# Query tile 5 of the B heads turned by VectorE and DRAM, and the order's offsets set per stage

## The chip, the core and the metric

The kernel runs on one core of a Trainium2 chip. The metric is the device time of one execution in microseconds. TensorE (PE) multiplies matrices and turns 128x128 blocks, VectorE (DVE), ScalarE (ACT) and GpSimd (POOL) work on elements, and SyncE (SP) issues every DMA of this kernel. Each engine takes its instructions in the order in which the program holds them.

## The reference, cut to what matters

One layer over 1024 prompt tokens and 32 sample tokens, model width 1024:

```python
u = rmsnorm(h, g_pre) @ w_in            # q k v g of A (8 heads x 64) and of B (8 heads x 64)
oA = band attention                     # softmax(q k / 8 + relative bias), own 64-frame chunk and 8 before it
oB = stick_breaking(q, k, v)            # strictly causal:
z = q @ k.T * ATTN_SCALE
log_beta = log_sigmoid(z)
log_1m = where(causal, log_sigmoid(-z), 0)
after = cumsum(log_1m, reverse=True) - log_1m
w = where(causal, exp(log_beta + after), 0);  o = w @ v
y = concat(oA * silu(gA), oB * silu(gB)) @ w_out
h = h + rmsnorm(y, g_post)
h = h + sigmoid(h @ w_ple_gate) * (p @ w_ple)
```

The outputs are y of both groups and their new keys and values. In the kernel the weight of stick-breaking is a product: sigmoid(z) times the running product of sigmoid(-z) from the right.

## The kernel before, in words

Every product runs in fp32r, with an operand split into a high and a low part where precision asks for it (names ending in h and l). The input projections are done column by column (`col_steps`), 128 columns of w_in for 1056 tokens in three chunks of 352, 24 matmuls a chunk (`mm_qA`, `mm_kB`, `mm_gB` and so on).

Attention runs pair by pair of heads, A and B in turn (`pairs`: A0, B0, A1, ... B3), two heads a pair, eight query tiles a head. For query tile i `scores(i)` makes the scores in PSUM (`S`, three banks). For B, ScalarE makes two sigmoids into `om` and `be`, VectorE runs the scan in `om`, and GpSimd multiplies into `be`. For A, VectorE adds the bias and takes the extremum, ScalarE takes exp, GpSimd scales. Then `weights_t(i)` must turn the weights, so that keys lie on the partitions. There are two ways:

- on TensorE: a transpose of each 128x128 block into PSUM (`ptw`, two banks), after which ScalarE copies the high part (`wTh`) and VectorE subtracts for the low part (`wTl`);
- for the query tiles in `ROUND`: VectorE transposes all 32x32 blocks of the tile into `om`, one DMA writes `om` to a scratch tensor in DRAM (`swap`), and four DMAs read it back into `be` with the blocks in their new places. ScalarE and VectorE then make `wTh` and `wTl` from `be`.

Before, `ROUND` holds tile 5 of A's heads and tiles 4 and 6 of B's. Tile i of a B head has i+1 blocks of 128 keys. `values(g)` multiplies the turned weights of queries 4g to 4g+3 with the values (`PV`). `om` and `be` lie in rings (`Arena`), so that a later tile's room waits for the last use of an earlier one.

`weave` sets the attention steps of a pair beside the projections that the next pair needs: it takes from the list whose share of done work is behind, weighed by `RATES`, with the estimates of `SPACE_S`, `SPACE_T` and `SPACE_V` for the attention steps. `with_sums` puts in sums of the late weights at the places of `SUMS_STEP`, `with_sample` the steps of the sample group at `SAMPLE_AT`. After attention come the last gates, then the output product `o` and the gate product `g`, each with seven block products.

No instruction is issued directly. `Recorder.add` notes each one with what it must wait for and a key, which is its place in the recording (and a class: `cls` for TensorE, `low` for the others). `order()` then plays the program through with assumed durations and gives each engine, whenever it is free, the ready instruction of the lowest key. So the key decides which of several ready instructions goes first. `AHEAD_OF` shifts the key of instructions by engine and name of the tile written: a negative number lets it go earlier, a positive one later. Before, it does not touch TensorE:

```python
if eng != "PE" and writes:
    name = str(writes[0].buf.name)
    kind = (eng, name[:next(...)])
    o.key = (o.key[0], o.key[1] + AHEAD_OF.get(kind, 0))
```

Names in the profile: every instruction has line 490, where the recorder emits it, so groups are told apart by tile names. A trailing A or B tells the mixer.

Of the kernel before, what the change touches and what calls it, by code (L numbers as in the profile page):

```python
# [25 lines left out]
SCALE = HD ** -0.5  # L26
NT = 9
AHEAD_OF = {
    ('ACT', 'L'): 100, ('ACT', 'Qfs'): 50, ('ACT', 'stq'): 400, ('ACT', 'x'): -50,
# [3 lines left out]
}  # L33

ROUND = {"A": ((5,),), "B": ((4,),(6,))}
LAG_T = 2
LAG_V = 2
SPACE_S = {'A': 0.1, 'B': 0}  # L40
SPACE_T = {'A': 0.4, 'B': 0.4}
SPACE_V = {'A': 0.05, 'B': 0.0}
PARTS = 4
BEHIND = 2
RATES = (0.96, 0.86, 0.92, 1.0, 1.0, 0.86, 1.12, 0.86)
PLE_LAG = 4.0


# [6 lines left out]
class View:  # L55


    def __init__(self, buf, steps, box, dims, shape):
        self.buf, self.steps, self.box, self.dims, self.shape = buf, steps, box, dims, shape
# [213 lines left out]
class Recorder:  # L273


    def __init__(self):
        self.with_table, self.old_table = [], []
        self.ops, self.cls, self.low, self.closed, self.turns = [], 0, 0, [], []
        self.tensor = Engine(self, "PE", "tensor")
        self.vector = Engine(self, "DVE", "vector")  # L280
        self.scalar = Engine(self, "ACT", "scalar")
        self.gpsimd = Engine(self, "POOL", "gpsimd")
        self.sync = Engine(self, "SP", "sync")
# [26 lines left out]
    def node(self, eng, what, args, kw, after):  # L310
        o = Op()
        o.eng, o.what, o.args, o.kw, o.after = eng, what, args, kw, after
        o.key = (self.cls if eng == "PE" else self.low, len(self.ops))
        o.shared, o.table = False, None
        self.ops.append(o)
        return o

    def add(self, eng, what, args, kw):
        writes, reads = [], []
        method = what[1] if isinstance(what, tuple) else ""  # L320
        for i, a in enumerate(args):
            if isinstance(a, (View, Raw, Segments)):
                (writes if i == 0 or (method == "tensor_tensor_reduce" and i == 7) else reads).append(a)
        for k, a in kw.items():
            if isinstance(a, (View, Raw, Segments)):
                (writes if k in ("out", "accum_out") else reads).append(a)
        o = self.node(eng, what, args, kw, set())
        for mine, write in ((reads, False), (writes, True)):
            for v in mine:
                b = v.buf  # L330
                hit = False
                for other, box, wrote in b.uses:
                    if other is not o and (write or wrote) and all(p < y and x < q for (p, q), (x, y) in zip(v.box, box)):
                        o.after.add(other)
                        hit = True
                if b.pool is not None:
                    if not hit:
                        o.after.add(b.place)
                    b.pool.ops.append(o)
                b.uses.append((o, v.box, write))  # L340
        if method == "activation" and args[2] in (AF.Exp, AF.Sigmoid):

            o.table = args[2]
            if self.with_table and self.with_table[-1].table != o.table:
                self.old_table, self.with_table = self.with_table, []
            self.with_table.append(o)
            o.after.update(self.old_table)
        if eng != "PE" and writes:
            name = str(writes[0].buf.name)
            kind = (eng, name[:next((i for i, x in enumerate(name) if x.isdigit() or x in "AB_"), len(name))])  # L350
            o.key = (o.key[0], o.key[1] + AHEAD_OF.get(kind, 0))
        o.busy, o.late = self.cost(eng, method, args, kw, writes, reads)
        if eng == "SP":
            o.pieces = max(self.pieces(v) for v in args[0:2])
        o.shared = eng == "POOL"
        if eng == "DVE":
            sbuf = [v for v in reads if isinstance(v, (View, Segments)) and not v.buf.psum and v.free() > 4]
            o.shared = len(sbuf) > 1 or (method == "tensor_copy" and len(sbuf) == 1 and not writes[0].buf.psum)
# [137 lines left out]
def stream_step(  # L496
# [6 lines left out]
    rec = Recorder()  # L503
# [29 lines left out]
    hnl = [hnp.tile([P, KD, CH], F32R, tag=f"hnl{c}", name=f"hnl{c}") for c in range(NCH)]  # L533
# [14 lines left out]
    masks = const.tile([P, NS], F32, tag="masks", name="masks")  # L548
    qsS = const.tile([P, 4, NS], F32, tag="qsS", name="qsS")
    ksS = const.tile([P, 4, NS], F32, tag="ksS", name="ksS")  # L550
# [310 lines left out]
    def attention(ab, p, h):  # L861
# [15 lines left out]

        together = {i: g for g in ROUND[ab] for i in g}
        whole, done_with = {}, []

        def cost(i):
            return i + 1 - lo_block(i)
# [104 lines left out]
        def reach(g, b):  # L987

            seen = [i for i in range(4 * g, 4 * g + 4) if lo_block(i) <= b <= i]
            return slice((seen[0] - 4 * g) * P, (seen[-1] + 1 - 4 * g) * P)  # L990
# [23 lines left out]
        for i in range(8):  # L1014
            out["S", i] = (0.107 * cost(i) + SPACE_S[ab], lambda i=i: scores(i))
            out["T", i] = (0.107 * cost(i) + SPACE_T[ab], lambda i=i: weights_t(i))
        for g in range(2):
            columns = sum(reach(g, b).stop - reach(g, b).start for b in range(4 * g + 4))
            out["V", g] = (0.00088 * columns + SPACE_V[ab], lambda g=g: values(g))
        return out  # L1020
# [328 lines left out]
    def weave(n, att, den):  # L1349
# [5 lines left out]
        while ia < len(att) or idn < len(den):  # L1355
            take_a = ia < len(att) and (idn >= len(den) or RATES[n] * pa / ta <= pd / td)
            if take_a and att[ia][2] and any(x in prep for x in att[ia][2]):
# [52 lines left out]
                sub(b[key], b["B11"], b[key], ALU.subtract)  # L1410
                dma(sum_dr[w][kt, 3], b[key])

    SUMS_STEP = {2: [8, 34], 4: [10, 28], 5: [8, 28], 6: [14, 28]}

    def with_sums(n, att, todo):
        out = list(att)
        for i, (w, kt) in enumerate(todo):
            out.insert(SUMS_STEP[n][i], (0.0, lambda w=w, kt=kt: sum_weights(w, kt), None))
        return out

    SAMPLE_AT = {2: [0, 10, 16, 23, 26, 27], 3: [4, 10, 15, 22, 27, 32], 6: [1, 10, 15, 22, 27, 32], 7: [1, 9, 15, 22, 23, 32]}

    def with_sample(n, att, steps):
        out = list(att)
        for at_, st in reversed(list(zip(SAMPLE_AT[n], steps))):
            out.insert(at_, (st[0], st[1], None))
        return out
# [8 lines left out]
    grow = at2.tile([1, D], F32, tag="tok", name="grow", bufs=2)  # L1436
# [3 lines left out]
    ple = Ple(True)  # L1440
# [56 lines left out]

    seq = attention_stream()
    for n in range(8):
        den = []  # L1500
        for j in range(*span[n + 1]):
            den += col_steps(j)
        att = seq[n, 0] + seq[n, 1]
        if pairs[n][1] % 2 == 1:
            att = with_sample(n, att, sample_attention(pairs[n][0], pairs[n][1] // 2))
        att = with_sums(n, att, SUMS_AT.get(n, ()))
        weave(n, att, den)
# [2 lines left out]


    rec.close(at_stack, at)
    fb = rec.pool(ctx, tc, name="fb", bufs=1)
    GP = fb.tile([P, D], F32, tag="GP", name="GP")
    L, R = HALF
# [17 lines left out]
    ple = Ple(False)  # L1533
# [265 lines left out]

    for m, (nm, src, group) in enumerate(sets):  # L1800
        last_set = m == len(sets) - 1
        state = [{}, {}]
        for n, prod in enumerate(ORDER):
            for pair, t in enumerate(group):
# [43 lines left out]
                if nm == "o":  # L1848
                    rec.low = -1
                    if prod == "P2":  # L1850
                        add(st["h1u"][:, L], st["p1"], bank, ALU.add)
                        st["u"].square(0, st["h1u"][:, L])
                    if prod == "P6":
                        add(up, st["p1"], bank, ALU.add)
                    if prod == "P7":
                        add(dn, up, bank, ALU.add)
# [13 lines left out]
                else:  # L1870
                    uu = st.get("uu")
                    if prod in ("P2", "P4") and pair == 0:
                        name = f"cc{m}{prod}"
                        if m == 2 and prod == "P4":
                            cc = at2.tile([P, 2, 512], F32, tag="stg", name=name, bufs=3)
                        elif m == 3 and prod == "P2":
                            cc = at0.tile([P, 2, 512], F32, tag="L0", name=name)
                        else:
                            cc = fb.tile([P, 2, 512], F32, tag="GP", name=name)
# [76 lines left out]
```

## Time and profile before

| | |
|---|---|
| median of 3 runs | 783.63 us (783.26 to 783.88) |
| the profiled execution | 783.64 us |
| its span, first to last instruction | 781.9 us |
| granted clock of TensorE, mean | 0.999 |
| busy: TensorE / VectorE / ScalarE / GpSimd | 98% / 77% / 68% / 60% |
| moved by DMA | 154.71 MB, mean 198 GB/s |

A row of the groups reads: line, engine, operation, tile written <- tiles read, shapes, count, then busy time in us and the mean ns of one, then the idle time of the engine just before them and what ended it. The busy time of TensorE contains matmuls that overlap; what one costs is read from start to start. A line of the timeline has start and length in us, then the instruction and the count of a run of equal ones. The stretch from 50 to 575 us holds the attention and most of the gates, that before it the norms and the first projections, that behind it the last gates and the output and gate products.

### The profile page before, as it was taken

How to read it: one execution, taken by the hardware profiler on the slowest of the kernel's cores; microseconds unless marked ns; L12 is line 12 of the kernel's file. 1: busy time of each engine (PE TensorE's matmuls, PEld its weight loads, DVE VectorE, ACT ScalarE, POOL GpSimd, SP SyncE). 2: the span in 40 equal slices, each digit the busy share in tenths (PEclk: the TensorE clock that was granted, in tenths of full speed). 3: DMA queues.
4: the chain of work that ended last, by engine and by line, in shares of the span. 5: the costliest groups of instructions: out<-in, count | busy, mean ns of one | idle time of the engine just before them, and what ended most of it. 6: DMA issues, size and time to landing. Idle time of an engine off the chain costs nothing.

```text
span 781.9 us, 14437 instructions
## 1 busy us (share of the span) xinstructions
PE 769.8 (98%) x4534; PEld 711.2 (91%) x4534; DVE 602.9 (77%) x1127; ACT 528.4 (68%) x1146; POOL 471.7 (60%) x551
## 2 busy tenths in 40 slices
PE   8999999999999999999999999999999999999997
PEld 6999999999999999999999999999998877877786
DVE  7827767888778888688988798888474687988965
ACT  5647775877786777787767777674347867685651
POOL 5636624574666446775966677575553438599533
PEclk9999999999999999999999999999999999999999
DMA  8657634557765638776757977775689856659754
GB/s 301 215 152 180 161 82 139 136 128 210 177 196 167 183 92 240 185 213 210 197 143 199 260 209 218 197 223 167 184 276 289 274 181 220 239 160 346 250 181 134
DMA packets 184542, 154.71 MB, mean 198 GB/s; under 512 B 64705, under 2 KB 150505, under 8 KB 184466
## 3 DMA queue, kind: packets, MB, share of 16 engines
q1 hardware_dynamic: 184466, 153.79, 66.8%
q8 instruction: 36, 0.59, 0.3%
q14 instruction: 40, 0.33, 0.1%
HBM read 94.97 MB, written 50.36 MB: 186 GB/s over the span
## 4 chain that ended last, share of the span: by engine, by line
PE 80%; POOL 7%; DVE 4%; DMA 3%; issue 3%; SPq 2%; ACT 1%; POOLq 0%; DVEq 0%; ACTq 0%
PE mm_gB L490 6%; PE mm_qB L490 6%; PE mm_qA L490 5%; PE mm_vA L490 5%; PE mm_kA L490 5%; PE mm_vB L490 5%; PE mm_kB L490 4%; PE PVB L490 4%; PE SB L490 4%; PE PVA L490 3%; PE SA L490 3%; PE ptwA L490 3%; PE o1P L490 3%; PE g2P L490 2%; PE o0P L490 2%
## 5 line engine op out<-in xcount | busy, mean ns | idle before, releaser
L490 POOL TENSOR_TENSOR be<-be,om 128x256 f32<-128x256 f32 (+8 forms) x66 | 83.5, 1269 | 82.1 <-DVE om L490 48.9
L490 DVE TENSOR_TENSOR_SCAN om<-om,SB 128x384 f32<-128x384 f32 (+5 forms) x96 | 92.6, 968 | 20.2 <-ACT be L490 11.1
L490 ACT ACTIVATE om<-SB 128x384 f32<-128x384 f32 (+5 forms) x96 | 46.6, 499 | 23.8 <-DVE SB L490 12.5
L490 POOL TENSOR_SCALAR be<-be,statA 128x640 f32<-128x640 f32 (+4 forms) x64 | 46.0, 727 | 25.8 <-DVE statA L490 22.2
L490 ACT ACTIVATE be<-SB 128x384 f32<-128x384 f32 (+5 forms) x96 | 46.3, 500 | 13.2 <-DVE om L490 6.6
L490 ACT ACTIVATE be<-om,statA 128x640 f32<-128x640 f32 (+4 forms) x64 | 44.4, 695 | 5.9 <-DVE statA L490 3.9
L490 DVE TENSOR_TENSOR wTl<-ptwA,wTh 128x512 fp32r<-128x512 f32 (+2 forms) x80 | 37.2, 482 | 12.5 <-ACT wTh L490 11.4
L490 ACT CAST wTh<-ptwA 128x512 fp32r<-128x512 f32 (+2 forms) x80 | 32.2, 425 | 20.4 <-PE ptwA L490 19.1
L490 ACT CAST wTh<-ptwB 128x512 fp32r<-128x512 f32 (+3 forms) x64 | 29.8, 488 | 15.4 <-PE ptwB L490 10.7
L490 DVE TENSOR_TENSOR wTl<-ptwB,wTh 128x512 fp32r<-128x512 f32 (+3 forms) x64 | 33.5, 542 | 5.3 <-ACT wTh L490 4.9
L490 PE MATMUL SB<-kdB,LB 128*128 128x384 f32 (+5 forms) x96 | 33.4, 353 | 0.4 <-DVE om L490 0.3
L490 PE MATMUL ptwA<-ident,be 128*128 128x128 f32 x200 | 33.2, 273 | 0.0
L490 DVE CUSTOM_DVE_ANT_0 om<-SA,biasA 128x320 f32<-128x320 f32 (+3 forms) x64 | 30.3, 482 | 3.6 <-PE SA L490 3.0
L490 PE MATMUL SB<-klB,LB 128*128 128x384 f32 (+5 forms) x96 | 32.5, 342 | 0.0
L490 PE MATMUL SA<-kdA,LA 128*128 128x320 f32 (+2 forms) x96 | 30.4, 320 | 0.1
L490 PE MATMUL ptwB<-ident,be 128*128 128x128 f32 x192 | 29.1, 274 | 1.3 <-POOL be L490 1.0
L490 DVE TENSOR_TENSOR wTl<-be,wTh 128x640 fp32r<-128x640 f32 (+1 forms) x24 | 29.1, 1211 | 1.0 <-ACT wTh L490 1.0
L490 PE MATMUL SA<-klA,LA 128*128 128x320 f32 (+2 forms) x96 | 29.9, 315 | 0.0
L490 POOL TENSOR_TENSOR gB<-gB,gB 128x256 f32<-128x256 f32 x32 | 26.0, 821 | 1.5 <-DMA gB<-in_w_ple_gate_dram 1.3
L490 PEld LDWEIGHTS ptwB<-ident,be 128*128 128x128 f32 x192 | 23.0, 140 | 3.1 <-POOL be L490 1.7
L490 POOL TENSOR_TENSOR klA<-stkA,kdA 64x1024 fp32r<-64x1024 f32 (+2 forms) x9 | 19.4, 2152 | 10.5 <-ACT kdA L490 10.2
L490 PEld LDWEIGHTS ptwA<-ident,be 128*128 128x128 f32 x200 | 24.8, 140 | 0.8
(696 smaller groups left out, 2667.5 us busy)
## 6 DMA issues: line engine op xcount, KB each, us to landing
oB<-in_w_out_dram SPq DMA_DIRECT2D x16, 256.0 KB, 3.6
sum_dro<-oB SPq DMA_DIRECT2D x16, 256.0 KB, 3.1
gB<-in_w_ple_gate_dram SPq DMA_DIRECT2D x16, 256.0 KB, 3.2
sum_drg<-gB SPq DMA_DIRECT2D x16, 256.0 KB, 2.3
x<-in_x_prompt_dram SPq DMA_DIRECT2D x16, 256.0 KB, 3.4
h_dr<-h SPq DMA_DIRECT2D x8, 512.0 KB, 3.6
ht<-h_dr SPq DMA_DIRECT2D x8, 512.0 KB, 4.4
raw<-sum_drg SPq DMA_DIRECT2D x16, 256.0 KB, 4.1
```

The source lines that it names most:

```text
L490: getattr(getattr(tc.nc, o.what[0]), o.what[1])(*args, **kw)
```

## The change

`ROUND["B"]` gets the group `(5,)`, so that tile 5 of each B head goes by VectorE and DRAM like 4 and 6, with a swap of its own. The offsets of the key are replaced by new ones, a second table gives further offsets by stage (the pair being woven, and the parts before and after it), both now hold for TensorE and for instructions that write no tile, and some estimates of `weave` and places of `with_sums` and `with_sample` get other numbers.

```diff
 AHEAD_OF = {
-    ('ACT', 'L'): 100, ('ACT', 'Qfs'): 50, ('ACT', 'stq'): 400, ('ACT', 'x'): -50,
-    ('DVE', 'Kl'): -100, ('DVE', 'cc'): 200, ('DVE', 'h'): -100, ('DVE', 'sq'): -75,
-    ('SP', 'be'): -50, ('SP', 'biass'): 200, ('SP', 'kd'): 50, ('SP', 'pl'): -25,
-    ('SP', 'ple'): 100, ('SP', 'pp'): -200, ('SP', 'sum'): -400,
+    ('ACT', 'L'): 85, ('ACT', 'kd'): 335, ('ACT', 'om'): -36, ('DVE', 'Kcs'): 131,
+    ('DVE', 'Kl'): 1158, ('DVE', 'L'): 85, ('DVE', 'Vh'): -64, ('DVE', 'Vl'): -126,
...
+    ('DVE', 'ot'): 166, ('DVE', 'w'): -194, ('PE', 'S'): 872, ('POOL', 'be'): -189,
...
+AHEAD_AT = {
+    (0, 'ACT', 'stv'): -1402, (0, 'DVE', 'v'): 727, (0, 'POOL', 'wph'): -310, (0, 'SP', 'grow'): 880,
...
+    (3, 'DVE', 'ot'): 284, (3, 'DVE', 'stats'): 488, (3, 'DVE', 'vx'): -1348, (3, 'PE', 'Ss'): 1489,
...
+    (8, 'SP', 'Kcs'): 582, (8, 'SP', 'be'): -293, (8, 'SP', 'ogg'): -88,
+}
-ROUND = {"A": ((5,),), "B": ((4,),(6,))}
+ROUND = {"A": ((5,),), "B": ((4,), (5,), (6,))}
-SPACE_S = {'A': 0.1, 'B': 0}
-SPACE_T = {'A': 0.4, 'B': 0.4}
-SPACE_V = {'A': 0.05, 'B': 0.0}
+SPACE_S = {'A': 0.15, 'B': 0}
+SPACE_T = {'A': 0.35, 'B': 0.4}
+SPACE_V = {'A': 0, 'B': 0}
-RATES = (0.96, 0.86, 0.92, 1.0, 1.0, 0.86, 1.12, 0.86)
+RATES = (1.0, 0.86, 0.92, 0.96, 0.96, 0.88, 1.14, 0.98)
-        o.key = (self.cls if eng == "PE" else self.low, len(self.ops))
+        o.key = (self.cls if eng == "PE" else self.low, len(self.ops), len(self.ops))
-        if eng != "PE" and writes:
-            name = str(writes[0].buf.name)
...
-            o.key = (o.key[0], o.key[1] + AHEAD_OF.get(kind, 0))
+        v = (writes or reads)[0].buf.name if writes or reads else ""
+        kind = eng, ("" if writes else "to ") + v[:next((i for i, x in enumerate(v) if x in "0123456789AB_"), len(v))]
+        n = o.key[2]
+        o.key = o.key[0], n + AHEAD_OF.get(kind, 0) + AHEAD_AT.get((self.stage, *kind), 0), n
-    SUMS_STEP = {2: [8, 34], 4: [10, 28], 5: [8, 28], 6: [14, 28]}
+    SUMS_STEP = {2: [8, 31], 4: [10, 26], 5: [3, 28], 6: [10, 28]}
-    SAMPLE_AT = {2: [0, 10, 16, 23, 26, 27], 3: [4, 10, 15, 22, 27, 32], 6: [1, 10, 15, 22, 27, 32], 7: [1, 9, 15, 22, 23, 32]}
+    SAMPLE_AT = {2: [0, 10, 16, 23, 26, 27], 3: [4, 10, 15, 22, 27, 32], 6: [1, 10, 15, 23, 27, 32], 7: [1, 9, 15, 22, 23, 32]}
     for n in range(8):
+        rec.stage = n + 1
     rec.close(at_stack, at)
+    rec.stage = 9
```

More of the change, by code (lines that the diff above doesn't have):

```diff
@@ L28 @@
 AHEAD_OF = {
-    ('ACT', 'L'): 100, ('ACT', 'Qfs'): 50, ('ACT', 'stq'): 400, ('ACT', 'x'): -50,
[3 rows of a table removed]
-}
-ROUND = {"A": ((5,),), "B": ((4,),(6,))}
+    ('ACT', 'L'): 85, ('ACT', 'kd'): 335, ('ACT', 'om'): -36, ('DVE', 'Kcs'): 131,
+    ('DVE', 'Kl'): 1158, ('DVE', 'L'): 85, ('DVE', 'Vh'): -64, ('DVE', 'Vl'): -126,
+    ('DVE', 'hnl'): 49, ('DVE', 'kt'): 150, ('DVE', 'newl'): -26, ('DVE', 'om'): -178,
+    ('DVE', 'ot'): 166, ('DVE', 'w'): -194, ('PE', 'S'): 872, ('POOL', 'be'): -189,
+    ('POOL', 'ksS'): -765, ('POOL', 'om'): 417, ('POOL', 'qsS'): 86, ('POOL', 'wl'): -54,
@@ new lines @@
+    ('SP', 'Kcs'): -383, ('SP', 'Vcs'): 705, ('SP', 'be'): 17, ('SP', 'grow'): -1084,
+    ('SP', 'masks'): -251, ('SP', 'pp'): -218, ('SP', 'stv'): -1085, ('SP', 'sum'): -400,
+}
+AHEAD_AT = {
+    (0, 'ACT', 'stv'): -1402, (0, 'DVE', 'v'): 727, (0, 'POOL', 'wph'): -310, (0, 'SP', 'grow'): 880,
+    (1, 'ACT', 'stv'): 403, (1, 'POOL', 'wl'): 829, (2, 'ACT', 'L'): -36, (2, 'ACT', 'be'): 27,
+    (2, 'ACT', 'wTh'): -1042, (2, 'ACT', 'wh'): -91, (2, 'DVE', 'L'): -186, (2, 'DVE', 'S'): -734,
+    (2, 'DVE', 'ot'): -104, (3, 'ACT', 'newh'): -1262, (3, 'ACT', 'om'): 555, (3, 'ACT', 'wTh'): -64,
[3 rows of a table added]
+    (4, 'ACT', 'be'): 43, (4, 'ACT', 'stk'): 918, (4, 'ACT', 'wh'): 75, (4, 'DVE', 'L'): -191,
[3 rows of a table added]
+    (6, 'ACT', 'be'): 27, (6, 'ACT', 'wTh'): 103, (6, 'DVE', 'S'): -14, (6, 'DVE', 'om'): 123,
+    (6, 'DVE', 'stat'): 71, (6, 'PE', 'PV'): 359, (6, 'SP', 'be'): 346, (6, 'SP', 'o'): 185,
+    (7, 'ACT', 'L'): 210, (7, 'ACT', 'newh'): -111, (7, 'ACT', 'wTh'): -307, (7, 'DVE', 'L'): -357,
+    (7, 'DVE', 'om'): -26, (7, 'DVE', 'ot'): -179, (7, 'DVE', 'stat'): -53, (7, 'DVE', 'wTl'): -121,
+    (7, 'PE', 'mm'): 108, (7, 'PE', 'ptw'): 1103, (7, 'SP', 'kl'): 716, (7, 'SP', 'swap'): -202,
+    (8, 'ACT', 'ot'): 774, (8, 'ACT', 'sgg'): -54, (8, 'DVE', 'Kcs'): -507, (8, 'DVE', 'Vl'): 62,
+    (8, 'DVE', 'newl'): 677, (8, 'DVE', 'om'): 110, (8, 'DVE', 'sgg'): 173, (8, 'PE', 'mm'): -54,
+    (8, 'SP', 'Kcs'): 582, (8, 'SP', 'be'): -293, (8, 'SP', 'ogg'): -88,
+}
@@ L276, in __init__ @@
     def __init__(self):
-        self.with_table, self.old_table = [], []
+        self.with_table, self.old_table, self.stage = [], [], 0
         self.ops, self.cls, self.low, self.closed, self.turns = [], 0, 0, [], []
@@ L347, in add @@
             o.after.update(self.old_table)
-        if eng != "PE" and writes:
-            name = str(writes[0].buf.name)
-            kind = (eng, name[:next((i for i, x in enumerate(name) if x.isdigit() or x in "AB_"), len(name))])
-            o.key = (o.key[0], o.key[1] + AHEAD_OF.get(kind, 0))
+        v = (writes or reads)[0].buf.name if writes or reads else ""
+        kind = eng, ("" if writes else "to ") + v[:next((i for i, x in enumerate(v) if x in "0123456789AB_"), len(v))]
+        n = o.key[2]
+        o.key = o.key[0], n + AHEAD_OF.get(kind, 0) + AHEAD_AT.get((self.stage, *kind), 0), n
         o.busy, o.late = self.cost(eng, method, args, kw, writes, reads)
@@ L1801, in stream_step @@
         last_set = m == len(sets) - 1
+        rec.stage = 10 + m
         state = [{}, {}]
```

5 rows, old and new, of the table AHEAD_AT are left out of this document.

## The prediction

> **What bounds the kernel now.** I read the page's busy times first, then the sums by stretch, then TensorE's own waits, then the timeline of TensorE around the step that goes. The page:
>
> ```profile
> span 781.9 us, 14437 instructions
> PE 769.8 (98%) x4534; PEld 711.2 (91%) x4534; DVE 602.9 (77%) x1127; ACT 528.4 (68%) x1146; POOL 471.7 (60%) x551
> PE 80%; POOL 7%; DVE 4%; DMA 3%; issue 3%; SPq 2%; ACT 1%; POOLq 0%; DVEq 0%; ACTq 0%
> ```
>
> TensorE (PE) has work 98% of the span and holds 80% of the chain that ended last. The change touches the stretch from the first attention head to the last gate, 50 to 575 us. Sums of that stretch (busy time and count of each engine, granted clock, DMA share, GB/s), then TensorE's waits in it:
>
> ```profile
> 50.00:575.00 525.00, 523.15 (x3358) 507.74 (x3357) 414.11 (x847) 368.12 (x826) 327.64 (x393) 1.00 0.66 181
> PE ptwB L490 <- POOL be L490: 1.0, 2, 0.8
> PE ptwB L490 <- DVE wTl L490: 0.3, 1, 0.3
> PE SB L490 <- DVE om L490: 0.3, 1, 0.3
> ```
>
> Of 525.00 us TensorE is idle for 1.85. So here the time is the sum of TensorE's instructions: what leaves its stream shortens the span, and what is moved to another engine is hidden as long as TensorE does not come to wait for it. VectorE (DVE) is busy 414.11/525.00 = 79%, ScalarE (ACT) 70%, GpSimd (POOL) 62%, the clock is full at 1.00.
>
> **The turns that leave TensorE.** Eight B heads lose the turn of query tile 5: six 128x128 blocks each, 48 transposes. One such run, and what stands around it:
>
> ```profile
> 126.47 0.80 PE L490 MATMUL mm_kA<-hnh,wh_kA 128*128 128x352 f32 x4
> 127.11 0.82 PE L490 MATMUL ptwB<-ident,be 128*128 128x128 f32 x6
> 127.68 0.90 PE L490 MATMUL mm_kA<-hnh,wh_kA 128*128 128x352 f32 x4
> 128.41 0.64 PE L490 MATMUL mm_kA<-hnh,wl_kA 128*128 128x352 f32 x3
> L490 PE MATMUL ptwB<-ident,be 128*128 128x128 f32 x192 | 29.1, 274 | 1.3 <-POOL be L490 1.0 <-DVE wTl L490 0.3
> ```
>
> Read by starts, since matmuls overlap: the six take 127.11 to 127.68, 0.57 us. The four projections behind them take 127.68 to 128.41, 0.73 us, where the same four ahead of them take 126.47 to 127.11, 0.64: another 0.09. One run costs 0.66 us, or 0.11 for each transpose; eight runs 8 x 0.66 = 5.3 us, all of it on the path. That is the first term.
>
> The group's last row gives a mean of 274 ns for one transpose, and the Trainium skill ("TensorE: Matmul & The Clock Gate", Part 4: PE-mode transpose) has about 275 ns for one in the context of a kernel; by that, as a price, 48 would be 13.2 us. The starts say that it is a latency which the next instruction overlaps, so the sum goes by 0.11. The skill also speaks against the change: "VectorE: DVE Perf Modes", Rules for kernel authors, leaves a 128x128 transpose to TensorE wherever PSUM can take the result, since VectorE turns only 32x32 blocks. By that rule the step would have stayed; where TensorE is the full engine, as the 98% shows, the price on VectorE counts only if it is waited for.
>
> **What the other engines take over.** Tiles 4 and 6 of the same heads already go this way (640 and 896 columns); tile 5 has 768, and I take the middle of the two:
>
> ```profile
> L490 DVE STREAM_TRANSPOSE om<-be 128x640 f32<-128x640 f32 x16 | 13.3, 832 | 0.1
> L490 DVE STREAM_TRANSPOSE om<-be 128x896 f32<-128x896 f32 x8 | 8.8, 1105 | 0.7 <-POOL om L490 0.6
> L490 DVE TENSOR_TENSOR wTl<-be,wTh 128x640 fp32r<-128x640 f32 x16 | 17.9, 1121 | 0.6 <-ACT wTh L490 0.6
> L490 DVE TENSOR_TENSOR wTl<-be,wTh 128x896 fp32r<-128x896 f32 x8 | 11.1, 1391 | 0.4 <-ACT wTh L490 0.4
> L490 DVE TENSOR_TENSOR wTl<-ptwB,wTh 128x512 fp32r<-128x512 f32 x32 | 21.2, 677 | 3.8 <-ACT wTh L490 3.5 <-PE PVB L490 0.4
> L490 DVE TENSOR_TENSOR wTl<-ptwB,wTh 128x256 fp32r<-128x256 f32 x16 | 6.6, 411 | 0.3 <-ACT wTh L490 0.3
> L490 ACT CAST wTh<-be 128x640 fp32r<-128x640 f32 x16 | 11.8, 735 | 0.0
> L490 ACT CAST wTh<-be 128x896 fp32r<-128x896 f32 x8 | 7.6, 946 | 0.0
> L490 ACT CAST wTh<-ptwB 128x512 fp32r<-128x512 f32 x32 | 18.5, 594 | 14.7 <-PE ptwB L490 10.2 <-PE PVB L490 4.5
> L490 ACT CAST wTh<-ptwB 128x256 fp32r<-128x256 f32 x16 | 6.2, 385 | 0.0
> swapB<-om SPq DMA_DIRECT2D x8, 448.0 KB, 3.7
> be<-swapB SPq DMA_DIRECT2D x32, 112.0 KB, 2.7
> swapB<-om SPq DMA_DIRECT2D x8, 320.0 KB, 3.0
> be<-swapB SPq DMA_DIRECT2D x32, 80.0 KB, 2.2
> L490 SPq DMA_DIRECT2D be<-swapB x64: 318/430/1312, 130.9 to 544.0; - x64
> L490 ACT ACTIVATE om<-SB 128x384 f32<-128x384 f32 x24 | 12.0, 499 | 4.9 <-DMA be<-swapB 2.0 <-PE SB L490 1.8 <-DVE SB L490 1.1
> L490 DVE TENSOR_TENSOR_SCAN om<-om,SB 128x384 f32<-128x384 f32 x24 | 23.2, 966 | 2.0 <-ACT be L490 1.4 <-ACT om L490 0.2
> L490 POOL TENSOR_TENSOR be<-be,om 128x768 f32<-128x768 f32 x8 | 12.4, 1551 | 13.9 <-DVE om L490 6.0 <-DMA swapB<-om 4.5 <-ACT be L490 3.4
> ```
>
> Per head VectorE gains (832+1105)/2 = 969 ns and (1121+1391)/2 = 1256, and loses 677+411 = 1088: +1.14 us, 9.1 us for eight heads. Its load in the stretch goes from 79% to (414.1+9.1)/520 = 81%. ScalarE gains 840 and loses 979: -0.14 us. SyncE's queue gets 5 issues a head, 40 x 0.43 = 17 us in 520, and the four reads stand behind the write's landing, so what is queued after them (loads of weights, stores) waits with them. DMA moves 2 x 384 KB more per head, 6.3 MB beside 525 us x 181 GB/s = 95 MB: its share goes from 0.66 to about 0.70.
>
> The new path is long: write about 3.4 us, reads 2.5, five issues 2.2, VectorE and ScalarE 3.1, together 11 us instead of the 2 us of casts and subtractions. It is read by the second value product of the head (queries 4 to 7). In the order of the changed program as built, 166 to 219 matmuls stand on TensorE between the last score matmul of tile 5 and that product; at 525.00/3358 = 0.156 us each, at least 26 us. Ahead of the turn lie four sigmoids of 384 columns (2.0 us), two scans (1.9) and GpSimd's product (1.6), 5.5 us, so some 9 us of cover are left: I cost the path at nothing. Should the cover go, TensorE waits for the excess in full. A gain beyond the 5.3 is possible too, since two PSUM banks of the turns come free earlier.
>
> **The order.** New offsets move instructions on every queue, and now TensorE's too. No row prices this; I compare the built orders. Between the last score matmul of a query tile and the first transpose of its weights stand more matmuls than before: median 92 for 80 in A's heads, 82 for 76 in B's. That is room for the softmax or the scan. TensorE's largest wait shows what room is needed:
>
> ```profile
> 172.61 1.27 PE L490 MATMUL mm_kB<-hnh,wh_kB 128*128 128x352 f32 x7
> 174.65 1.09 PE L490 MATMUL ptwB<-ident,be 128*128 128x128 f32 x8 [0.77 <-POOL be L490]
> ```
>
> Seven projections (0.16 us each) end their turn at 173.73; tile 7's transposes start at 174.65: 0.92 us lost, of which the view shows 0.77 as idle. There 50 matmuls stood between; the change makes it 53, and in two other heads 61 becomes 83 and 51 becomes 62, but in B's first head 105 shrinks to 51. The removed runs of tile 5 stood at 37 to 49 in seven heads, among the tightest. So idle time understates waits; from 0.92 against 0.77, and shorter waits that leave no idle row, I estimate 2 to 5 us of waits in the stretch. Bounds for this term: all of them vanish (-5), or the new tight places add as much again (+5). I take -1.3, nearer to none than to either end, for the longer distances.
>
> **Sum.** The profiled execution took 783.64 us (span 781.9), the median of the runs is 783.63, so no correction: 783.6 - 5.3 - 1.3 = 777.0 us. The first 50 us, and what follows 575 us, keep TensorE's order almost exactly; I cost them at nothing.
>
> **Rivals.**
>
> *VectorE's blocks stall TensorE (slower).* Each head puts a 0.97 us transpose and a 1.26 us subtraction into VectorE's in-order queue, ahead of scans that free score banks and feed GpSimd:
>
> ```profile
> POOL be L490 <- DVE om L490: 48.9, 21, 6.0
> ```
>
> For it: GpSimd already waits 48.9 us on scans. Against it: only 0.3 us of this reaches TensorE as idle. With 16 such blocks the gain is gone at 5.3/16 = 0.33 us of TensorE wait each, and the kernel is slower by 0.2% at 0.43. At 0.6 each: 783.6 - 5.3 + 9.6 = 787.9. Chance 0.13.
>
> *The new order gives the gain back.* The tight first head and moved S and T steps add 3 to 6 us of waits beside the 5.3 that go: about 783. For it: 105 to 51. Against it: most distances grew. Chance 0.09.
>
> *The order takes nearly all waits away.* -5.3 - 5 = 773.3. For it, the medians above; against it, waits of the same kind remain at 44 to 53 matmuls. Chance 0.18.
>
> *A transpose costs its whole 274 ns* (it blocks the stream): 48 x 0.274 = 13.2 us, 770.4. The starts in the timeline speak against it. The page on TensorE named above gives that figure. Chance 0.03.
>
> The forecast itself has 0.57.
>
> **How the numbers follow.** A measurement of this kernel can tell about 0.2% (1.6 us) from no change. Below 782.0 lie the forecast, the two rivals below it and a little of the give-back: 0.79; within 0.2% 0.08; slower 0.13. The range leaves out 0.08 below (part of the two large gains) and 0.10 above (most of the stall case): 771.5 to 785.5.
>
> **What would show it.** Right: TensorE's busy time in the attention stretch shorter by about 5 us, ptwB x144 in place of x192, the rest of TensorE's instructions the same, idle of TensorE in the stretch still under 3 us, VectorE near 81%. Wrong: waits of TensorE on DVE om, POOL be or a swap's DMA of over 4 us together, or the second value product waiting for the swapped weights; then the path of the swap or VectorE's queue sets the end. If the stretch is shorter by 5 us and the whole is not, the later stages waited for something else than TensorE.

## The result, and the profile after

The changed kernel takes 780.37 us (median of 4 runs, 779.57 to 781.02) where the kernel before took 783.75 (4 runs, 783.26 to 784.68): a ratio of 0.9955, 95% interval 0.9938 to 0.9972. Two later comparisons (e1 and e11 below) gave 0.9974 [0.9965, 0.9984] and 0.9971 [0.9960, 0.9983], so a gain of 2.4 to 3.4 us. The forecast was 777.0, a gain of 6.6.

The page's first lines, the engine line of the chain, and the sums of the stretch from 50 to 575 us, for the changed kernel (its operations carry line 514):

```profile
span 777.8 us, 14437 instructions
PE 766.0 (98%) x4486; PEld 707.2 (91%) x4486; DVE 599.8 (77%) x1127; ACT 529.0 (68%) x1138; POOL 476.2 (61%) x551
PE 76%; POOL 6%; DVE 6%; DMA 4%; issue 3%; ACT 2%; SPq 1%; POOLq 0%; DVEq 0%; ACTq 0%
50.00:575.00 525.00, 522.56 (x3332) 506.84 (x3331) 415.48 (x849) 368.74 (x819) 334.11 (x395) 1.00 0.70 194
```

TensorE has 48 instructions fewer and is still the engine that sets the end; its idle time in the stretch is 525.00 - 522.56 = 2.44 us (1.85 before). VectorE's load there is 415.48/525 = 79%, DMA's share 0.70. The groups that changed, by form, and the transfers of tile 5 (KB each, median us to landing):

```profile
L514 PE MATMUL ptwB<-ident,be 128*128 128x128 f32 x144 | 22.0, 273 | 0.1
L514 DVE STREAM_TRANSPOSE om<-be 128x768 f32<-128x768 f32 x8 | 7.8, 971 | 0.9 <-POOL be L514 0.7 <-POOL om L514 0.2
L514 DVE TENSOR_TENSOR wTl<-be,wTh 128x768 fp32r<-128x768 f32 x8 | 9.3, 1168 | 0.0
L514 ACT CAST wTh<-be 128x768 fp32r<-128x768 f32 x8 | 6.7, 838 | 0.0
swapB<-om SPq DMA_DIRECT2D x8, 384.0 KB, 2.8
be<-swapB SPq DMA_DIRECT2D x32, 96.0 KB, 3.1
```

TensorE's waits in that stretch (total, times, longest, in us):

```profile
PE SB L514 <- DVE om L514: 1.5, 1, 1.5
PE mm_qA L514 <- ACT stqA L514: 0.3, 1, 0.3
PE SsB L514 <- DVE QlsB L514: 0.2, 1, 0.2
PE mm_kB L514 <- ACT stvA L514: 0.2, 1, 0.2
```

The 1.3 us for GpSimd's and VectorE's weights (ptwB) of before are gone, and a single wait of 1.5 us for a score bank has come. It is at 379.5 us, and the timeline (start, duration) shows what it hangs on:

```profile
376.52 3.14 DVE L514 TENSOR_TENSOR wTl<-be,wTh 128x640 fp32r<-128x640 f32 x1
376.61 2.36 POOL L514 TENSOR_TENSOR be<-be,om 128x1024 f32<-128x1024 f32 x2
379.58 0.68 DVE L514 TENSOR_TENSOR SB<-SB,maskb 128x128 f32<-128x128 f32 x3
379.90 0.38 ACT L514 ACTIVATE om<-SB 128x256 f32<-128x256 f32 x1 [2.65 <-DVE SB L514]
380.64 2.64 DVE L514 TENSOR_TENSOR_SCAN om<-om,SB 128x256 f32<-128x256 f32 x3 [0.39 <-issue]
381.38 0.41 PE L514 MATMUL SB<-kdB,LB 128*128 128x320 f32 x1 [1.53 <-DVE om L514]
```

A subtraction that takes 0.80 us elsewhere took 3.14, ending 0.7 us after GpSimd's two products; the masks stood behind it, ScalarE's sigmoid behind the masks, the scan behind the sigmoid, and TensorE's next score matmul behind the scan. The stretching itself is not new: in the kernel before the longest of these subtractions, at 380.1 us, took 2.70 us and had two masks behind it, but no wait of TensorE over 0.5 us follows it there. New is what it holds up.

**A ledger of TensorE.** Idle rows leave short delays out, so I added up TensorE's starts instead, from the first k projection for the B heads (63.4 us) to the first output projection (604.2 us before, 600.5 after). Each matmul is charged the pitch that its width has undisturbed (160 ns for 352 columns, 230 for 512; a transpose 109 ns, the last of a run 28, and 85 more for the matmul behind the run). What a matmul with a semaphore wait takes beyond that is a wait; what the others take beyond it is "other", spread thinly over many matmuls; what causes it is not taken apart here. All matmuls but the transposes come to 482.4 us in every kernel here. The columns on the right are in us:

| kernel | median us (runs) | ratio to before, 95% | stretch | turns | waits | other |
|---|---|---|---|---|---|---|
| before | 783.75 (4) | 1 | 540.8 | 45.6 | 5.0 | 7.8 |
| after | 780.37 (4) | 0.9955 [0.9938, 0.9972] | 537.1 | 40.3 | 5.6 | 8.8 |
| e1 after again | 781.70 (9) | 0.9974 [0.9965, 0.9984] | 538.7 | 40.3 | 6.9 | 9.0 |
| e11 after, third time | 781.01 (7) | 0.9971 [0.9960, 0.9983] | 537.8 | 40.3 | 6.1 | 9.0 |
| e2 route alone | 798.26 (4) | 1.0188 [1.0174, 1.0202] | 555.4 | 40.3 | 21.2 | 11.4 |
| e3 offsets alone | 790.54 (5) | 1.0091 [1.0077, 1.0105] | 546.6 | 45.6 | 9.4 | 9.2 |
| e4 subtraction 6 behind | 779.75 (5) | 0.9953 [0.9940, 0.9967] | 537.0 | 40.3 | 5.5 | 8.8 |
| e5 turns doubled (before) | 786.74 (5) | 1.0037 [1.0023, 1.0051] | 544.7 | 50.9 | 4.4 | 7.1 |
| e6 blocks doubled (after) | 786.17 (7) | 1.0036 [1.0025, 1.0048] | 542.5 | 40.3 | 9.9 | 9.8 |
| e7 route alone, blocks thin | 799.37 (4) | 1.0201 [1.0186, 1.0215] | 553.9 | 40.3 | 20.8 | 10.3 |
| e8 subtraction 4 behind | 780.44 (5) | 0.9958 [0.9945, 0.9971] | 537.2 | 40.3 | 5.5 | 9.0 |
| e9 route, order held | 796.56 (4) | 1.0167 [1.0153, 1.0181] | 553.6 | 40.3 | 21.9 | 9.0 |
| e10 turns, order held | 789.53 (5) | 1.0075 [1.0063, 1.0088] | 546.9 | 45.6 | 9.7 | 9.2 |
| e12 e9 with thin blocks | 789.85 (5) | 1.0084 [1.0070, 1.0097] | 547.0 | 40.3 | 15.5 | 8.7 |

In the three profiles of the changed kernel the turns are 5.3 us shorter, waits are longer by 1.2 on the mean and other by 1.1: 2.9 us net.

### The profile page after: what moved, and what is told of

It is laid out like the page before. It is cut to its first block, busy times and chain, and to the rows that moved or that the text cites. A ratio compares the mean times of both kernels' runs of the same rounds, so it can differ in the third digit from the quotient of the medians.

```text
span 777.8 us, 14437 instructions
## 1 busy us (share of the span) xinstructions
PE 766.0 (98%) x4486; PEld 707.2 (91%) x4486; DVE 599.8 (77%) x1127; ACT 529.0 (68%) x1138; POOL 476.2 (61%) x551
## 4 chain that ended last, share of the span: by engine, by line
PE 76%; POOL 6%; DVE 6%; DMA 4%; issue 3%; ACT 2%; SPq 1%; POOLq 0%; DVEq 0%; ACTq 0%
PE mm_vB L514 6%; PE mm_qB L514 6%; PE mm_gB L514 6%; PE mm_kB L514 6%; PE mm_kA L514 6%; PE mm_vA L514 5%; PE SB L514 4%; PE PVB L514 4%; PE PVA L514 4%; PE mm_qA L514 4%; PE SA L514 3%; PE mm_gA L514 3%; PE ptwA L514 3%; PE g2P L514 2%; PE g3P L514 2%
## 5 line engine op out<-in xcount | busy, mean ns | idle before, releaser
L514 POOL TENSOR_SCALAR be<-be,statA 128x640 f32<-128x640 f32 (+3 forms) x64 | 45.1, 717 | 28.1 <-DVE statA L514 12.8
L514 DVE TENSOR_TENSOR wTl<-ptwA,wTh 128x512 fp32r<-128x512 f32 (+3 forms) x80 | 36.9, 481 | 6.9 <-ACT wTh L514 5.5
L514 ACT CAST wTh<-ptwA 128x512 fp32r<-128x512 f32 (+3 forms) x80 | 31.6, 426 | 12.5 <-PE ptwA L514 10.8
L514 DVE TENSOR_TENSOR wTl<-be,wTh 128x640 fp32r<-128x640 f32 (+2 forms) x32 | 36.7, 1152 | 2.3 <-ACT wTh L514 2.0
L514 DVE CUSTOM_DVE_ANT_0 om<-SA,biasA 128x320 f32<-128x320 f32 (+4 forms) x64 | 29.9, 479 | 6.2 <-PE SA L514 4.1
L514 DVE STREAM_TRANSPOSE om<-be 128x640 f32<-128x640 f32 (+2 forms) x32 | 30.0, 937 | 4.5 <-POOL be L514 4.2
L514 DVE TENSOR_TENSOR wTl<-ptwB,wTh 128x512 fp32r<-128x512 f32 (+3 forms) x48 | 25.3, 545 | 7.4 <-ACT wTh L514 6.9
L514 POOL TENSOR_TENSOR oB<-oB,oB 128x256 f32<-128x256 f32 x32 | 24.8, 795 | 7.2 <-DMA oB<-in_w_out_dram 7.2
L514 ACT CAST wTh<-be 128x640 fp32r<-128x640 f32 (+2 forms) x32 | 25.9, 811 | 4.1 <-DMA be<-swapB 3.1
L514 ACT CAST wTh<-ptwB 128x512 fp32r<-128x512 f32 (+3 forms) x48 | 22.1, 487 | 8.2 <-PE ptwB L514 6.1
```

The costliest lines, as they stand in the source:

```text
L514: getattr(getattr(tc.nc, o.what[0]), o.what[1])(*args, **kw)
```

## The experiments

**e1, the changed kernel again, with e2 to e4 on one chip.** No edit.

> The changed kernel itself, timed beside the next three on one chip, so that they can be compared with it. Both theories: 780.4 us, ratio to the kernel before 0.9955.

Measured 781.70; the wait at 379 us is there again (1.8 us in the ledger).

**e2, the route alone.** The kernel before, its offsets untouched:

```diff
-ROUND = {"A": ((5,),), "B": ((4,),(6,))}
+ROUND = {"A": ((5,),), "B": ((4,), (5,), (6,))}
```

> The kernel before with the group (5,) in ROUND of B and nothing else; the order is planned anew with the old offsets. Theory A (TensorE's stream is the bound; the 48 transposes pay 5.3 us, and 1.6 us of it came back through the new offsets): 783.7 - 5.3 = 778.4, with 2 us either way for waits that the new plan makes. Theory B (the transposes are worth only the 3.4 us that were seen, since the waits before them went with them, and the offsets did nothing): 780.4. Theory C (the way through DRAM costs what it saves, the gain came from the offsets): 783.7 or more. TensorE's start-to-start account should again show 5.3 us less for transposes in every case.

Measured 798.26, 14 us slower than before. Theories A and B fail; of C only the words "or more" cover it, and none had a reason for 14 us. The turns fell to 40.3 us as the forecast said, but TensorE's waits rose from 5.0 to 21.2. Its longest waits in the stretch, and the worst of its stretched subtractions, this time for tile 5 itself (VectorE, then GpSimd beside it, then TensorE behind it):

```profile
PE SB L490 <- DVE om L490: 3.1, 3, 2.6
PE ptwB L490 <- DVE wTl L490: 1.9, 1, 1.9
PE SA L490 <- DVE statA L490: 1.7, 3, 1.0
388.51 4.57 DVE L490 TENSOR_TENSOR wTl<-be,wTh 128x768 fp32r<-128x768 f32 x1
390.15 2.12 POOL L490 TENSOR_TENSOR gB<-gB,gB 128x256 f32<-128x256 f32 x3
393.83 0.30 PE L490 MATMUL ptwB<-ident,be 128*128 128x128 f32 x1 [1.92 <-DVE wTl L490]
```

Not all of the 14 us is waiting. The mean granted clock was 0.993 to 0.996 in all runs of e2 and 0.991 to 0.996 in those of e7, where the kernel before had 0.998 to 1.000 beside them. In e2's profile the clock (third number from the end of these sums) falls to a half three times, for 3.4 us each, twice within 1.3 us behind the two longest waits:

```profile
217.60:221.00 3.40, 3.01 (x11) 3.01 (x12) 2.43 (x13) 2.11 (x5) 2.85 (x3) 0.50 0.78 227
275.60:279.00 3.40, 3.40 (x10) 2.72 (x9) 2.44 (x6) 2.39 (x6) 3.40 (x3) 0.50 0.49 145
395.10:398.50 3.40, 3.40 (x14) 3.36 (x14) 2.13 (x4) 2.37 (x5) 3.25 (x4) 0.50 0.73 171
```

At half the clock these three cost at most 3 x 1.7 = 5.1 us; by the ledger's pitches it is about 4.5, of which 2.1 stand under waits and 2.4 under other. No other kernel of the table but e7 (two of them) has such a stretch before its last 10 us.

**e3, the offsets alone.** The changed kernel with the old ROUND line, so that TensorE turns tile 5.

> The changed kernel with tile 5 of B's heads turned by TensorE again: new offsets, old ROUND. Theory A: the offsets alone are a loss of about 1.6 us, 785.3 (784 to 787). Theory B: 783.7. Theory C: about 780.

Measured 790.54, 6.4 us slower than before and above all three theories; waits 9.4 us. The offsets are no gain by themselves. Each half of the change costs; only both together gain.

**e4, the stretched subtraction later.** The changed kernel; in the planned order, the subtraction that took 3.14 us is moved behind six further VectorE instructions (low weights of one block of one head change with it):

```diff
+        j = (the subtraction wTlB20_1 <- beB20_4)
+        late = ops.pop(j)
+        for _ in range(6):
+            j = next(k for k in range(j, len(ops)) if ops[k].eng == "DVE") + 1
+        ops.insert(j, late)
```

> The changed kernel with one VectorE instruction moved: the subtraction for tile 4 of head 20, which took 3.1 us beside a GpSimd product and stood ahead of three score masks and three scans, goes behind those three scans. Theory A: TensorE's wait of 1.7 us at 379.5 us goes and nothing comes in its place: 1.6 us less than the changed kernel, 778.8, a ratio near 0.9935. Rival: the wait only moves (to the value product that reads the subtraction, or to the next scores): 780.4.

Measured 779.75, 1.95 us less than e1 on the same chip, and the wait at 379 us is gone: this chain, from subtraction to score bank, is shown for its place. A wait of 1.0 us has come at 385 us, for ScalarE's rounding of tile 6 behind its four reads from DRAM. As a gain the 1.95 us is weak: e4's ratio to the kernel before, 0.9953, is also that of the changed kernel in its first comparison, 0.9955.

**e5, turns doubled.** The kernel before with each of tile 5's 48 transposes issued twice (the condition is given in words).

```diff
-                    getattr(getattr(tc.nc, o.what[0]), o.what[1])(*args, **kw)
+                    for _ in range(2 if (a TensorE transpose into ptwB.._5) else 1):
+                        getattr(getattr(tc.nc, o.what[0]), o.what[1])(*args, **kw)
```

> The kernel before, order untouched, with each of the 48 TensorE transposes of tile 5 of B's heads issued twice in a row (the second writes the same values again). It measures by itself what a transpose costs in its place. Theory of the prediction's first step (each costs its pitch of about 0.11 us, a run of six 0.66 us with its changeover, which is not paid twice here): +48 x 0.109 = +5.2 us, so about 789 beside a before of 784. Rival (each costs the 0.274 us that a transpose shows as its duration): +13 us, so about 797. If banks of PSUM come late behind the longer turns: more than 5.2 with new rows 'PVB' or 'SB' among TensorE's waits.

```profile
L491 PE MATMUL ptwB<-ident,be 128*128 128x128 f32 x240 | 34.3, 273 | 1.0 <-POOL be L491 1.0
```

The turns grew by 5.2 us, from 45.6 to 50.9, which is 0.109 us each and not the 0.273 of the row's mean. The time grew by less: the stretch by 3.9, since waits and other fell by 1.3, and the median of the runs by 3.1 (interval 1.8 to 4.0). So a part of what these transposes take was time that TensorE lost anyway. The ledger rests on one profile of each kernel here, and e5's is of its slowest run.

**e6, VectorE's blocks doubled.** The changed kernel with its eight 128x768 VectorE transposes issued twice, by the same kind of edit: +7.8 us of VectorE.

> The kernel after, order untouched, with each of the 8 VectorE transposes of tile 5 of B's heads (0.97 us each) issued twice: +7.8 us of VectorE at the places that the change gave it, nothing else. Theory of the prediction's second step (VectorE's work on tile 5 hides behind TensorE, some 9 us of cover left behind each): at most +1 us, 780 to 782.5 where after had 780.4 and 781.7. Rival (VectorE's blocks stall TensorE, of which the one wait of 1.7 us at 379.5 would be the first sign): 0.2 to 0.5 us for each block, +1.6 to +4 us, 783 to 786, with longer rows 'SB <- DVE om' or 'ptwB <- DVE wTl' among TensorE's waits.

```profile
L515 DVE STREAM_TRANSPOSE om<-be 128x768 f32<-128x768 f32 x16 | 15.6, 976 | 1.2 <-POOL be L515 0.7 <-POOL om L515 0.2
PE SB L515 <- DVE om L515: 2.8, 4, 1.6
PE SA L515 <- DVE om L515: 0.6, 1, 0.6
PE SB L515 <- DMA swapB<-om: 0.5, 1, 0.5
```

Measured 786.17. With the changed kernel at 0.997 of before, 0.0066 x 783.6 = 5 us more, 0.65 for each block of 0.97: most of it reaches TensorE, as waits (9.9 for 6.2 us). So at these eight places VectorE, at 79%, has no room left for a block that the order does not expect. It is not a price of VectorE's time alone: the doubled block also lets the swap's write start 0.97 us later, and the last row above is a wait for that write. This is the rival, with a price above what it had named.

**e7, the route alone with thin blocks.** e2, of tile 5's blocks VectorE handles 128 columns of 768.

```diff
+                        if o.what[1] == "transpose":
+                            args[0:2] = args[0][:, 0:1], args[1][:, 0:P]
+                        elif five[0].startswith("wTl"):
+                            args[0:3] = [x[:, :, 0:1] for x in args[0:3]]
```

> The new route with the old offsets as in e2_route_alone (798.3 us), its planned order untouched, but of tile 5's blocks VectorE turns and subtracts only 128 of 768 columns, 16 instructions cut by a total of some 16 us; the rest of these blocks' turned and low weights isn't computed. TensorE, ScalarE, GpSimd, SyncE and the DMAs do what they did. Theory V (VectorE's added work is what stalls TensorE in that order: its waits there grew from 5.0 to 21.2 us): waits fall to 8 to 11 us, the time to 785 to 789. Theory O (the order planned with unfitted offsets is what stalls it, wherever VectorE's work lies): only the 1.9 us behind the one subtraction of 4.57 us goes, waits stay at 16 to 20 us, the time at 793 to 797.

Measured 799.37, no less than e2, with waits at 20.8: 14.7 us of VectorE's time taken away (these 16 instructions took 20.0 us in e2, 5.3 here) brought nothing in that order. Net it was less: VectorE's busy time fell from 606.7 to 598.1 us, since other subtractions grew. Taking the clock's stretches out of both (4.5 us in e2's profile, 3.0 in e7's) does not part them either: waits without them are 19.1 and 19.4 us. Theory V fails here. The 1.9 us that should have gone did not go either: the subtraction for tile 4 took its place, 5.05 us long beside the same products.

**e8, the subtraction four behind.** As e4, but only past three masks and one scan; nothing else moves.

> The kernel after with one VectorE instruction moved: the subtraction for tile 4 of the fifth head that took 3.14 us beside GpSimd's products, at 376.5 us, now stands behind the next three masks and one scan of the following head, and nothing else moves; all is computed. In e4_sub_behind it stood two scans further behind, and part of one block of low weights was changed by that; there the wait of 1.7 us at 379.5 went, another of 1.0 us came at 384.8, and the time fell by 1.95 us beside after on the same chip. Theory (the stretched subtraction holds up the masks and so the score bank): the wait at 379.5 goes, 778.5 to 780.5, 1 to 2 us less than after. Rival (the GpSimd products hold whatever VectorE instruction with two operands in SBUF comes next to them, and the subtraction is late for ptwB or PVB instead): within 0.5 us of after.

The same stretch in VectorE's timeline:

```profile
378.44 0.65 DVE L526 TENSOR_TENSOR SB<-SB,maskb 128x128 f32<-128x128 f32 x2 [0.76 <-PE SB L526]
379.46 0.68 DVE L526 TENSOR_TENSOR_SCAN om<-om,SB 128x256 f32<-128x256 f32 x1
380.05 0.80 DVE L526 TENSOR_TENSOR wTl<-be,wTh 128x640 fp32r<-128x640 f32 x1
PE SsB L526 <- DVE QlsB L526: 0.6, 1, 0.6
PE SB L526 <- ACT be L526: 0.4, 1, 0.4
```

The subtraction takes 0.80 us now, and the wait at 379 us shrank from 1.7 to 0.6 us in the ledger. The time, 780.44, is in the expected range, but not apart from the changed kernel: 0.9958 [0.9945, 0.9971] here, 0.9955 to 0.9974 for the other in three comparisons. Of the other waits, one of 0.5 us at 322.5 grew; the 0.7 us ahead of the sample's scores (SsB) at 503.7 are in the changed kernel too, at 0.3 to 0.7 in its three profiles. A better version is not shown.

**e9, the route in the held order.** e2 and e3 replan everything, so they mix the route with a new order. Here the planned order of the kernel before is kept for all operations that both kernels have: it is written into the kernel as a list, with the eight heads' new operations put in at fixed distances behind the product.

```diff
-        ops = self.order()
+        recorded = list(self.ops)
+        self.order()
+        ops = [recorded[i] for i in held]
```

> The new route for tile 5 of B's heads in the order of the kernel before, which is not planned anew: the planned places of all operations that both kernels have are kept (a handful of GpSimd, SyncE and ScalarE operations slide by a few places where a buffer comes free later), the 48 TensorE transposes with their ScalarE and VectorE evictions are gone, and behind each head's product the VectorE transposes stand 1.7 us on by the planner's clock, the write 3.1 us, the four reads 8 us, ScalarE's rounding 17 us and VectorE's subtraction 18.2 us. It separates the route from the new order, which route_alone changed together. Theory O (the order planned with unfitted offsets cost the 15 us, not the route): TensorE's transposes go from 45.6 to 40.3 us, waits stay at 5 to 7 us, 778 to 781. Theory V (the route's VectorE blocks stall TensorE, at the 0.6 us a block that e6 paid): waits of 9 to 11 us, 783 to 785. Theory W (the path over DRAM is late for the values): new rows PVB <- ACT wTh or <- DVE wTl, over 785.

```profile
PE SB L720 <- DVE om L720: 5.7, 8, 1.7
PE SsB L720 <- DVE om L720: 1.6, 1, 1.6
PE PVA L720 <- DVE v2A L720: 1.6, 1, 1.6
POOL om L720 <- DMA swapB<-om: 13.3, 4, 5.0
```

Measured 796.56. Theory O falls: with TensorE's and VectorE's order exactly as before, the route alone brings waits from 5.0 to 21.9 us. Theory V's place (scans late for score banks) holds for the largest row, 5.7 us in eight waits, but that is a third of the 16.9 us that came, and its size was too small. W is wrong: no value product waits over 0.4 us for swapped weights. The places of the new operations are one choice, at fixed distances; 13 us is the route's price with them, not with the best ones. The last row is new: GpSimd stands 13.3 us ahead of the memset that is the first use of an om buffer, since the buffer is free only when the swap's write has landed. The kernel before has no such wait, and the changed kernel has 2.9 us of it.

**e10, TensorE's turns in the held order after.** The reverse: the changed kernel's order as a list, tile 5's transposes put back.

> The reverse: TensorE turns tile 5 of B's heads again, in the order of the kernel after, with its offsets and nothing planned anew: its six transposes stand where VectorE's block stood (0.3 us on by the planner's clock), the evictions right behind. Theory O: after plus what the 48 transposes cost in a fixed order, 3.1 us (e5) to 5.2 us (their pitch): 783.5 to 787, and waits near after's 5.6 us. Theory V: VectorE is relieved by 0.6 us a block, which gives 3 to 5 us of that back: 779 to 782.5. If the fitted offsets are good for both routes alike, it comes out at or under the kernel before; if only for the new route, above it.

```profile
PE SB L745 <- DVE om L745: 1.7, 1, 1.7
PE ptwB L745 <- DVE wTl L745: 1.6, 1, 1.6
```

Measured 789.53, above both theories and above the kernel before, so the fitted offsets are good for the new route alone: the turns are back at 45.6 us, and waits are 9.7 although VectorE has less to do. With e11 the four corners on one chip are: old order and old route 783.49, old order and new route 796.56, new order and old route 789.53, both new 781.01. The route costs 13.1 us in the old order and gains 8.5 in the new one.

**e11, the changed kernel on that chip.** No edit.

> The kernel after as it is, once more, for a comparison with e9 and e10 on the same chip: 780 to 782.

Measured 781.01.

**e12, e9 with thin blocks.** The edit of e7 in the held order.

> e9_route_held (796.6 us, TensorE's waits 21.9 us) with its order, its buffers, its DMAs and its waits as they are, but of tile 5's blocks VectorE turns and subtracts only 128 of 768 columns, which takes some 13 us of VectorE's time away; the rest of these blocks' turned and low weights isn't computed. Theory V (the busy time of the new VectorE instructions in a queue that is full around them is what makes scans and masks late): waits fall to 7 to 11 us, 782 to 786. Theory B (what counts is not how long they run but what they hold: the om buffer until the write has landed, for which GpSimd stood 13.3 us before a memset where before it had no such wait, the be buffer until the subtraction, for which ScalarE stood 5.6 us where before 2.5): waits stay at 16 to 21 us, 791 to 796. In between, both.

```profile
PE SB L726 <- DVE om L726: 3.1, 5, 1.1
PE SsB L726 <- DVE om L726: 1.0, 1, 1.0
POOL om L726 <- DMA swapB<-om: 16.2, 5, 5.2
```

Measured 789.85: in between. Of the 16.9 us of waits that the route added, 6.4 (21.9 to 15.5) go with 10.7 us of VectorE's blocks (16.8 to 6.1). The other 10.5 stay when the blocks are nearly gone, and GpSimd's wait for the om buffer stays with them (16.2 us). That what the route holds, rather than how long it runs, makes up these 10.5 us is argued from that row, not shown: no run gave om and be longer rings. Nor is it settled why the same cut brought nothing in e2's order.

## Why the prediction was right or wrong

**The bound** held: TensorE idles 2.4 us of 525 after the change, and every kernel here follows its ledger.

**The turns, -5.3 us,** came out exactly: 45.6 to 40.3 us. The rival of 274 ns a transpose is out by e5. What the prediction left out is that a transpose can fill time that is lost anyway: in a fixed order 48 more cost 3.1 to 3.9 us, not 5.2. Whether 48 fewer also gain less than their pitch no run shows by itself, since the route came with it each time.

**The sizes** of the moved work were right: 971 and 1168 ns for 969 and 1256, ScalarE 838 for 840, the write 2.8 us for 3.4, each read 3.1 for 2.5, DMA's share 0.70 for 0.70, VectorE 79% for 81. The swapped weights were hardly late for the second value product, as its long cover said: in the three profiles of the changed kernel by at most 0.4 us at a time, the longest for tile 6.

**"Hidden, hence nothing" is the step that was wrongly reasoned.** It weighed VectorE's mean load and the cover of the path, and neither was the limit. What counts in part is that scans free score banks, and that VectorE's queue is full around them: e6 puts 0.65 us on a further block, and e9 13 us on the whole route where the order was not made for it, of which e12 gives 6.4 us of waits to VectorE's busy time. The rest of the 13 us stays open. The prediction had this as its rival of 0.13, with 787.9. Its mechanism is there; it did not decide, because the offsets, which the prediction took for a small separate term, remove nearly all of it. The sign that the prediction had named, idle rows of over 4 us together, would not have told: the changed kernel has 1.5 us of them, while the ledger's waits rose. Nor can a window of a fixed 525 us show TensorE busy 5 us less, since later work moves into it (523.15 and 522.56 us); the turns had to be added up.

**The order, -1.3 us, is the term that was mis-sized, and in sign:** together with the path that was costed at nothing it measured +2.4 (1.2 of waits, the rest other) in the changed kernel. With the longer distances between scores and transposes the waits for B's weights did go, from 2.1 to 0.4 us in the ledger, but those for score banks rose from 1.2 to 2.5, 1.7 of it at a single tight place on VectorE. The waits before, which the prediction estimated at 2 to 5 us, are 5.0 in the ledger. As a separate term it does not exist: the new order costs 6 us with the old route (e10) and saves 15.6 with the new one (796.6 to 781.0). The case "gives the gain back" (3 to 6 us, 783) was nearer in size than the forecast, but through a subtraction on VectorE held up beside GpSimd and not through the first head, where 105 matmuls had become 51 and no wait showed.

So: -5.3 + 2.4 = -2.9 in the stretch where -6.6 was forecast, and the time fell by 2.4 to 3.4 us. The direction came from the turns. The miss of 3.7 us lies in the terms of nothing and of -1.3 together, and no run splits it between them. That the time still lies well inside 771.5 to 785.5 is in part luck: what hid the work was a fitted order and not the cover that was argued, and with the old order the same route takes 797 to 798 us.

## What to carry to other kernels

When an instruction leaves the full engine, count its pitch by starts and not its duration, and expect less than that, since some of it may have covered waits (here 48 added transposes cost 3.1 us of time for 5.2 of pitch). Work that goes to an in-order queue is hidden only if what stands behind it there can wait too: look at who frees the full engine's banks, not at the mean load. And where a planned order has been fitted to one route, a new route can be judged only with its own fit: here each half of the change alone lost 6 to 14 us, and both together gained 2.4 to 3.4.

## What the runs showed of the hardware

A VectorE subtraction with two operands in SBUF stands still while GpSimd runs a product, and in most places it waits for that one product alone, even when another follows at once. In the changed kernel, a subtraction of 896 columns, 1.07 us alone, began at 534.96, ended 0.95 us behind the product that was running, and held up the next one, which took 1.79 us where its like take 0.94:

```profile
533.15 2.55 POOL L514 TENSOR_TENSOR wl_gB<-wr_gB,wh_gB 128x512 fp32r<-128x512 f32 x2 [1.95 <-ACT wh_gB L514]
534.96 1.70 DVE L514 TENSOR_TENSOR wTl<-be,wTh 128x896 fp32r<-128x896 f32 x1
535.67 1.79 POOL L514 TENSOR_TENSOR sggA<-sggA,oggA 128x352 f32<-128x352 f32 x1
```

Of the subtractions from `be` in the 14 profiles, 138 took more than a quarter over the shortest of their width, and 127 of these waited only for the GpSimd instruction that was running. In the other 11, all of the same head and one in each of 11 profiles, further products began while the subtraction stood: 3.14 us (0.80 alone) in the changed kernel, ending 0.7 us behind two of them; 4.57 (0.95 alone) in e2, ending 0.8 behind the last of five; 5.05 in e7, 0.7 behind the last of six, although memsets stood between some of them. It came out at 3.14 or 3.15 in all five profiles that kept the order of the kernel after there. Why it was passed over at this place stays open.

The Trainium skill ("SBUF — State Buffer", Who interferes with whom) says that a VectorE instruction with two SBUF inputs contends with a GpSimd one that reads SBUF, and (SBUF: two separate sides) that the loser blocks for the whole instruction; the traces agree in the 127, and at this one place it was several instructions.

A run of transposes on TensorE starts one every 109 ns although each shows 273, and the matmul behind the run takes 85 ns more: 0.11 us net for each in runs of six.
